# A two-layer diffusion backbone on one core: modulation column on TensorE, Fourier sums on VectorE, urgencies for the pieces of the first phase

## The chip, the cores and the metric

The program runs on one core of a Trainium2 chip. The metric is the device time of one execution in microseconds (us), and the lower the better. A "time" below is the median of the timed runs unless it is called the profiled execution's own.

## What is computed

The reference carries a latent stream `x` (512 tokens, width 1024) through two layers and a final norm; all is fp32.

```python
# each layer: modulated norm, mixer, gated residual; then the same with the MLP
h = modulate(rmsnorm(x, norm1_g[i]), sh1, sc1)     # h * (1 + scale) + shift
y = hybrid_ab_mixer(...) if even else fourier_mixer(h, fourier_w_out[j])
x = x + gt1 * y
x = x + gt2 * channel_mlp(modulate(rmsnorm(x, norm2_g[i]), sh2, sc2), w1[i], w2[i])
# channel_mlp: square(relu(h @ w1)) @ w2,  w1 1024 x 4096
# fourier_mixer: real part of fft2 over (tokens, 256 channels of a group), then a 1024 x 1024 map
# hybrid mixer: input projection -> windowed attention with 256 context keys, and a
#               bidirectional RWKV-7 scan (chunks of 64 tokens) -> output projection
return rmsnorm(x, final_g)
```

The shifts, scales and gates come from `silu(c) @ ada_w + ada_b`.

## The kernel before

The body does not issue instructions; it records them. A `Plan` object notes every operation (`record`), knows what each must wait for, and then orders all of them in `solve`: it steps through a model of the five engines and takes, on each engine, the ready operation with the largest urgency, which is the length of the longest chain of work behind it plus the record's `lead` (0 for all records in the kernel before). `issue` then writes the instructions in that order, so each engine runs its own list strictly in order. Where the plan's model sees TensorE wait, it puts in dummy matmuls, `warm<-identr` (L673), that keep TensorE busy. All instructions come from that one place, so nearly every row of the profile says L683; rows are told apart by their tiles.

Every fp32 product is made of three matmuls (`mm3`): an operand is split into a high part (ScalarE, `whi<-st`, `hhi<-ht`, `uhi<-x`) and the rest (VectorE, `wlo<-st,whi`, `hlo`, `ulo`). Weights arrive by SyncE's queue as 128 x 512 halves in the ring `st` (five buffers); `whi` and `wlo` have three buffers each.

The stages in order of time:

- First phase, 0 to about 560 us. A table of words, `PLAN`, lists its pieces: `tile` (a tile of the input projection, matmuls `ps<-hhi,whi`), `post`, `lora`, `ada` (columns of the modulation, made on VectorE), `prep`, `mats`, `nat`, `inv` (inversion of 64 x 64 blocks, with the small matmuls `Yt,ab`, `Vt,Zt`, `Xs,ab` and `ab,Xs`), the scan chain `u`, `s`, `y` (`vu,ab`, `zs,ab`, `vu,gq`, `St`), attention (`qry`, `max`, `row`, `attn`) and the output projection (`out`, `read`).
- Layer 0's MLP, 590 to 920 us. `norm_rows` sums the squares (`ps<-cst,sq`), makes the reciprocal root (VectorE `ms`, GpSimd `rs`) and spreads it over the partitions (`ps<-cst,rs`, ScalarE `rb`). Only then can `mod_split` make the modulated input: VectorE `ht<-x,AM,rb`, ScalarE `hhi`, VectorE `hlo`, for eight tiles of 128 channels.
- So that TensorE need not wait for that, the first `NG` tiles of the MLP take the unnormalised input (`uhi`, `ulo`) and are scaled by `rb` after their matmuls. The shift of the modulation then has to be added as a column, `w1` transposed times the shift: GpSimd multiplies the weight tile by the shift (`wb<-st,adv`), adds the eight parts up (`wb<-wb`), and TensorE sums over the partitions with one matmul against a column of ones (`ps<-cst,wb`); ScalarE copies the result to `wbs`.
- The Fourier layer, 920 to 1018 us. `fw_load` makes the sum `wa` (GpSimd) and the difference `wb` (VectorE) of two weight halves, `fw_split` splits both; `PF` is how many output tiles ahead they are made. For each of eight output tiles, ScalarE makes `qg` from one product, GpSimd subtracts and adds it to the residual (`xn<-xn,qg`), VectorE adds the other product (`x<-ps,adv,xn`), and ScalarE and VectorE split the result for the MLP.
- Layer 1's MLP, from 1018 us, in which `last` makes the final norm in two halves of 256 tokens: eight products `o<-y,rb` a half, of which GpSimd makes those of `PLM`.

Of the kernel before, what the change touches and what calls it, by code (L numbers as in the profile page):

```python
# [8 lines left out]
ALU = mybir.AluOpType  # L9
# [229 lines left out]
class Plan:  # L239
# [11 lines left out]
    def __init__(self, nc):  # L251
        self.nc = nc
        for e in self.ENGS:
            setattr(self, e, Queue(self, e))
        self.recs, self.pools, self.closed = [], [], []
        self.tiles, self.hist, self.preds, self.soft = {}, {}, [], []
        self.ahead, self.piece = 0, 0


    def tile_pool(self, **kw):  # L260
# [431 lines left out]
def body(tc, I, out):  # L692
# [4 lines left out]
    act, dve, pool, pe = nc.scalar, nc.vector, nc.gpsimd, nc.tensor  # L697
# [22 lines left out]
    ones1 = K("ones")  # L720
# [638 lines left out]
    y = {}  # L1359
# [399 lines left out]


    PLAN = """
    tile 0, tile 1, post 0, lora 0, tile 2, post 1, lora 1, tile 3, post 2, lora 2, tile 4, post 3, lora 3, tile 5,
    ada 2, post 4, prep 0 0, ada 4, prep 0 1, tile 6, post 5, mats 0 0, mats 0 1, nat 0 0, nat 0 1,
    inv 0, tile 7, ada 6, post 6, tile 8, ada 8, post 7, ada 10, tile 9, tile 10, ada 12, post 8, post 9, tile 11,
    ada 14, post 10, tile 12, ada 16, post 11, rope, tile 14, post 12, prep 1 0, prep 1 1,
    mats 1 0, mats 1 1, nat 1 0, nat 1 1, tile 15, post 14, inv 1, tile 16, ada 18, post 15,
    prep 2 0, prep 2 1, mats 2 0, mats 2 1, nat 2 0, tile 17, ada 20, post 16, tile 18, ada 22,
    tile 19, post 17, inv 2, post 18, ada 24, nat 2 1, tile 13, post 19, post 13, kv, u 0 0, s 0 0,
    u 0 1, s 0 1, prep 3 0, prep 3 1, u 1 0, s 1 0, mats 3 0, mats 3 1, nat 3 0,
    nat 3 1, inv 3, qry 0, max 0 0, u 1 1, max 0 1, row 0, s 1 1, prep 4 0,  # L1770
    bonus 2, prep 4 1, mats 4 0, mats 4 1, nat 4 0, nat 4 1, inv 4, ed 2 0,
    ed 2 1, u 2 0, s 2 0, y 2 0, u 2 1, s 2 1, y 2 1, prep 5 0, prep 5 1, mats 5 0, mats 5 1, nat 5 0, inv 5,
    attn 0, bonus 3, ed 3 0, ed 3 1, u 3 0, s 3 0, y 3 0, u 3 1, s 3 1, y 3 1, qry 1,
    max 1 0, max 1 1, row 1, u 4 0, s 4 0, ed 4 0, ed 4 1, y 4 0, bonus 4, u 4 1, attn 1,
    qry 3, max 3 0, ed 5 1, y 4 1, s 4 1, u 5 0, s 5 0, ed 5 0, max 3 1, row 3,
    bonus 5, y 5 0, u 5 1, y 5 1, attn 3, qry 2, max 2 0, max 2 1, row 2, attn 2, out 0,
    out 1, out 2, out 3, out 4, out 5, out 6, out 7, read 4, read 5, read 3, read 2
    """
# [55 lines left out]
    def tq(name, shape=(128, 512)):  # L1834
        return h2("E", shape=shape, name=name)


    NG = 3
    PF = 3
    AXE = 1  # L1840

    def mlp(l, xs, ai, sh, gt, nxt):

        us = US[:]
        US.clear()

        rb = norm_rows(Q, SQ, T, "rk")
        gs = []
        for f in range(NG):
            st = load(I["w1"][l, f])  # L1850
            pr = [tq("wb") for u in range(2)]
            for u in range(2):
                b = adv[:, sh + 4 * u : sh + 4 * u + 4].unsqueeze(2).to_broadcast([128, 4, 128])
                pool.tensor_tensor(pr[u].rearrange("p (k c) -> p k c", k=4), st[u].rearrange("p (k c) -> p k c", k=4), b, ALU.mult)
            w = split_w(st)
            p = pst("ch" if f < 2 else "iv")
            for k in range(8):
                mm3(p, w, k, us[k], k == 0, k == 7)
            pool.tensor_tensor(pr[0], pr[0], pr[1], ALU.add)
            for n in (256, 128):  # L1860
                pool.tensor_tensor(pr[0][:, 0:n], pr[0][:, 0:n], pr[0][:, n : 2 * n], ALU.add)
            pb = pst("rk")
            pe.matmul(pb[:, 0:1], pr[0][:, 0:128], ones1, start=True, stop=True)
            wb = Q.tile([128, 1], F32, tag="wbs", bufs=NG, name="wbs")
            act.copy(wb, pb[:, 0:1])
            gs.append((p, wb))
        hs = []
        for k in range(8):
            hi, lo = hq("hhi"), hq("hlo")
            mod_split(Q, xs[k], rb, AM[:, ai, k : k + 1], adv[:, sh + k : sh + k + 1], hi, lo, T)  # L1870
            hs.append((hi, lo))
        for half in range(2):
            zs = []
            for f in range(16):
                if l == 0:
                    ada_bg(24 + max(0, 32 * half + f - 3) * 56 // 60)
                r = tq("r")
                if half == 0 and f < NG:
                    dve.tensor_tensor(r, gs[f][0], rb, ALU.mult)
                    act.activation(r, r, AF.Relu, bias=gs[f][1])  # L1880
                else:
                    w = split_w(load(I["w1"][l, 16 * half + f]))
                    p = pst("mm")
                    for k in range(8):
                        mm3(p, w, k, hs[k], k == 0, k == 7)
                    act.activation(r, p, AF.Relu)
                s = tq("s")
                act.activation(s, r, AF.Square)
                hi, lo = zq("zhi"), zq("zlo")
                act.copy(hi, s)  # L1890
                dve.tensor_tensor(lo, s, hi, ALU.subtract)
                zs.append((hi, lo))
            nx = []
            for m in range(8):
                if l == 1 and half == 1 and m == 6:
                    ws = [wk for kh in range(2) for wk in split_w(load(I["w2"][l, half, 7, kh]), True)]
                if l == 1 and half == 1 and m == 7:
                    return last(ws, zs, xs[m], adv[:, gt + m : gt + m + 1])
                p = pst("mm")
                for kh in range(2):  # L1900
                    if l == 0:
                        ada_bg(24 + (32 * half + 13 + 2 * m + kh) * 56 // 60)
                    w = split_w(load(I["w2"][l, half, m, kh]))
                    for k in range(8):
                        mm3(p, w, k, zs[8 * kh + k], kh == 0 and k == 0, kh == 1 and k == 7)
                xn = xt("xn")
                dve.scalar_tensor_tensor(xn, p, adv[:, gt + m : gt + m + 1], xs[m], ALU.mult, ALU.add)
                nx.append(xn)
                if half == 1:
                    nxt(xn, m)  # L1910
            xs = nx
        return xs
# [33 lines left out]
    def fw_load(m):  # L1946
        st = load(I["fw"][m])
        wa, wb = h2("ed", name="wa"), h2("ed", name="wb")
        pool.tensor_tensor(wa, st[0], st[1], ALU.add)
        dve.scalar_tensor_tensor(wb, st[0], K("onez"), st[1], ALU.mult, ALU.subtract)  # L1950
        return wa, wb

# [86 lines left out]
    for m in range(8):  # L2039
        if m + PF < 8:  # L2040
            fou["w", m + PF] = fw_load(m + PF)
            fw_split(m + PF)
        w = fou["ws", m]
        pq, pp = pst("mm"), pst("mm")
        for g in range(4):
            mm3(pq[:, 0:256], w, 4 + g, U[g][1], g == 0, g == 3)
        for g in range(4):
            mm3(pp[:, 0:258], w, g, U[g][0], g == 0, False)
        ms = slice(128 * (m % 4), 128 * (m % 4) + 128)
        fxh, fxl = fx[m // 4]  # L2050
        pe.matmul(pp[:, 0:258], fxh[:, ms], uxh, start=False, stop=False)
        pe.matmul(pp[:, 0:258], fxh[:, ms], uxl, start=False, stop=False)
        pe.matmul(pp[:, 0:258], fxl[:, ms], uxh, start=False, stop=True)
        gt = adv[:, 48 + m : 49 + m]
        qg = tq("qg", (128, 256))
        act.activation(qg, pq[:, 0:256], AF.Copy, scale=gt)
        xr = x2[m]
        pool.tensor_tensor(xr[:, 1:256], xr[:, 1:256], qg[:, 1:256], ALU.subtract)
        pool.tensor_tensor(xr[:, 257:512], xr[:, 257:512], qg[:, 255:0:-1], ALU.add)
        xn = xt("x3")  # L2060
        dve.scalar_tensor_tensor(xn[:, 0:256], pp[:, 0:256], gt, xr[:, 0:256], ALU.mult, ALU.add)
        dve.scalar_tensor_tensor(xn[:, 256:512], pp[:, 256:0:-1], gt, xr[:, 256:512], ALU.mult, ALU.add)
        x3.append(xn)
        scaled(xn, 2, m)
# [45 lines left out]
                dmae[q % 2].dma_start(out[g * q : g * q + g, :, c].rearrange("m p t -> p m t"), o)  # L2110

    PARTS = ((0, 256), (256, 256))
    PLM = (0, 2, 4)
    mlp(1, x3, 2, 56, 72, pre_final)
    p2.close()
    es.close()
# [20 lines left out]
```

## Time and profile before

| | |
|---|---|
| median of 3 timed runs | 1395.5 us (1393.81 to 1397.6) |
| profiled execution's own time | 1390.24 us |
| its span | 1388.5 us |
| mean granted TensorE clock | 0.971 |
| TensorE busy (matmul) | 1319.0 us, 95% |
| VectorE busy | 837.4 us, 60% |
| ScalarE busy | 613.2 us, 44% |
| GpSimd busy | 161.6 us, 12% |

The share of TensorE counts the dummy matmuls as busy, and matmuls that run at a lower clock count longer. So its 95% does not say that 5% is all there is to gain. The stretches are read one by one.

### The profile page before, as it was taken

The numbers are of one execution on the slowest core, as the hardware profiler recorded it, in microseconds if no ns is written. First come the engines' busy times: TensorE is split into PE (matmuls) and PEld (weight loads), VectorE is DVE, ScalarE is ACT, GpSimd is POOL, SyncE is SP. The second block draws the span as 40 slices with busy tenths as digits, with TensorE's granted clock in tenths as the row PEclk, the third lists the DMA queues.
The fourth block names the chain that finished last, engine by engine and source line by source line (L and its number), as shares of the span: only waits on it lengthen the run. The fifth ranks groups of instructions, "written<-read, shape, count | busy, mean of one in ns | idle before, by whom it ended". The sixth has DMA issues, their size and how long they took to land.

```text
span 1388.5 us, 27641 instructions
## 1 busy us (share of the span) xinstructions
PE 1319.0 (95%) x10824; PEld 1084.8 (78%) x10824; DVE 837.4 (60%) x1702; ACT 613.2 (44%) x1193; POOL 161.6 (12%) x219
## 2 busy tenths in 40 slices
PE   6999997789898999999999999999999999999997
PEld 2888885577777778778887888889978888888886
DVE  2874987678676456867555565675865332333334
ACT  3674744175533334537422455334537522355332
POOL 1420101122010111040000000000550000000001
PEclk9999997789998999999999999999999999999998
DMA  9488876746636113236655556570322333233222
GB/s 364 161 239 259 284 206 182 202 113 188 170 92 166 60 50 118 69 100 220 187 182 186 178 192 189 189 232 19 102 69 89 94 99 100 91 99 98 96 88 76
DMA packets 173938, 204.69 MB, mean 147 GB/s; under 512 B 52008, under 2 KB 87912, under 8 KB 173808
## 3 DMA queue, kind: packets, MB, share of 16 engines
q1 hardware_dynamic: 171920, 200.99, 46.8%
q8 instruction: 85, 1.39, 0.4%
q10 hardware_dynamic: 1376, 1.90, 0.4%
q14 instruction: 45, 0.37, 0.1%
q0 software_dynamic: 512, 0.03, 0.0%
HBM read 177.41 MB, written 25.43 MB: 146 GB/s over the span
## 4 chain that ended last, share of the span: by engine, by line
PE 57%; DVE 1%; DMA 1%; ACT 0%; issue 0%; POOL 0%; DVEq 0%; ACTq 0%
PE ps L683 55%; PE warm L673 1%; DMA st<-adaB_in 1%; DVE wlo L683 1%; DVE ht L683 0%; DVE st L683 0%; DVE o L683 0%; POOL o L683 0%; DVE xn L683 0%; ACT hhi L683 0%; ACT whi L683 0%; DVEq L2132 0%; ACT rb L683 0%; POOL rs L683 0%; DVE adv L683 0%
## 5 line engine op out<-in xcount | busy, mean ns | idle before, releaser
L683 ACT CAST whi<-st 128x512 fp32r<-128x512 f32 x306 | 188.2, 620 | 426.1 <-PE ps L683 365.6
L683 DVE TENSOR_TENSOR wlo<-st,whi 128x512 fp32r<-128x512 f32 x306 | 213.2, 707 | 213.4 <-ACT whi L683 154.4
L683 PE MATMUL ps<-hhi,whi 128*128 128x512 f32 x600 | 232.8, 399 | 7.6 <-ACT wbs L683 3.8
L683 PE MATMUL ps<-hlo,whi 128*128 128x512 f32 x600 | 230.7, 395 | 0.0
L683 PE MATMUL ps<-hhi,wlo 128*128 128x512 f32 x600 | 230.3, 398 | 0.0
L683 PE MATMUL ps<-zhi,whi 128*128 128x512 f32 (+1 forms) x528 | 200.2, 383 | 0.0
L683 PE MATMUL ps<-zlo,whi 128*128 128x512 f32 (+1 forms) x528 | 199.7, 383 | 0.0
L683 PE MATMUL ps<-zhi,wlo 128*128 128x512 f32 (+1 forms) x528 | 196.1, 384 | 1.8 <-DVE wlo L683 1.7
L683 PEld LDWEIGHTS ps<-hhi,whi 128*128 128x128 f32 x600 | 114.1, 191 | 34.2 <-ACT whi L683 5.7
L683 PEld LDWEIGHTS ps<-hhi,wlo 128*128 128x128 f32 x600 | 114.1, 190 | 23.9 <-DVE ab L683 0.5
L683 PEld LDWEIGHTS ps<-hlo,whi 128*128 128x128 f32 x600 | 114.0, 190 | 23.1 <-issue 0.9
L683 PEld LDWEIGHTS ps<-zhi,wlo 128*128 128x128 f32 x528 | 98.9, 188 | 22.7 <-DVE wlo L683 3.4
L683 PEld LDWEIGHTS ps<-zhi,whi 128*128 128x128 f32 x528 | 98.9, 188 | 20.0 <-ACT whi L683 0.7
L683 PEld LDWEIGHTS ps<-zlo,whi 128*128 128x128 f32 x528 | 99.1, 188 | 19.3
L683 DVE CUSTOM_DVE_ANT_0 st<-st,sB,vec 128x512 f32<-128x512 f32 x56 | 42.0, 750 | 44.2 <-DMA st<-adaB_in 43.8
L683 DVE TENSOR_TENSOR zlo<-s,zhi 128x512 fp32r<-128x512 f32 x64 | 43.9, 690 | 27.2 <-ACT zhi L683 27.2
L683 POOL TENSOR_TENSOR rs<-ms,pw 128x4 f32<-128x4 f32 (+1 forms) x7 | 6.2, 885 | 406.6 <-DVE ms L683 406.6
L683 POOL TENSOR_TENSOR wa<-st 128x512 f32<-128x512 f32 x8 | 11.6, 1452 | 341.2 <-DMA st<-fw_in 320.9
L683 DVE CUSTOM_DVE_ANT_0 st<-st,sB,adv 128x512 f32<-128x512 f32 x56 | 41.9, 748 | 9.3 <-DMA st<-adaB_in 8.4
L683 PE MATMUL ps<-pr,gq 64*128 64x128 f32 (+1 forms) x384 | 35.5, 302 | 6.6 <-DVE gq L683 5.1
L683 PEld LDWEIGHTS ps<-pr,gq 64*128 64x128 f32 x384 | 32.2, 206 | 11.3 <-issue 8.0
L683 ACT ACTIVATE s<-r 128x512 f32<-128x512 f32 x64 | 40.7, 636 | 0.6
(398 smaller groups left out, 2430.6 us busy)
## 6 DMA issues: line engine op xcount, KB each, us to landing
st<-w_in SPq DMA_DIRECT2D x256, 256.0 KB, 2.8
st<-adaB_in SPq DMA_DIRECT2D x112, 256.0 KB, 3.1
ada<-adaB_in SPq DMA_DIRECT2D x48, 256.0 KB, 3.9
st<-win_in SPq DMA_DIRECT2D x40, 256.0 KB, 4.2
spl_th<-th SPq DMA_DIRECT2D x16, 384.0 KB, 4.0
pgth<-spl_th SPq DMA_DIRECT2D x24, 256.0 KB, 4.8
st<-adaA_in SPq DMA_DIRECT2D x16, 256.0 KB, 5.0
st<-adaA_in SPq DMA_DIRECT2D x8, 512.0 KB, 7.5
```

What stands on the lines that cost most here:

```text
L673: i = tc.nc.tensor.matmul(p, i, i.unsqueeze(1).to_broadcast([128, 4, 128]), start=True, stop=True)
L683: i = getattr(getattr(tc.nc, r.eng), r.op)(*[tr(a) for a in r.args], **{x: tr(a) for x, a in r.kw.items()})
```

## The change

- `NG` 3 becomes 2: two tiles of each MLP, not three, use the unnormalised input. Their column is made by TensorE alone: eight matmuls `ps<-adv,st` (weights 128 x 128 as stationary operand, one column of the shift moving) instead of GpSimd's products and sums and one matmul.
- `PF` 3 becomes 4: the Fourier weights are made one output tile further ahead.
- The sum `wa` of `fw_load` and the two updates of the residual by `qg` move from GpSimd to VectorE.
- `PLM` becomes empty: all products of the final norm are on VectorE.
- The words of `PLAN` may carry a lead in us ("post 8:25.8"), which is added to the urgency of that piece's records. Some forty words carry one, between -60.6 and 27.2. What is recorded ahead of the table has a lead of 56.7 us, what comes behind it none.

```diff
-        self.ahead, self.piece = 0, 0
+        self.ahead, self.piece = 56700, 0
...
-    prep 2 0, prep 2 1, mats 2 0, mats 2 1, nat 2 0, tile 17, ada 20, post 16, tile 18, ada 22,
+    post 15, prep 2 0, prep 2 1, mats 2 0, mats 2 1:1.0, nat 2 0, tile 17, ada 20, post 16, tile 18, ada 22, tile 19,
...
     for piece in PLAN.replace("\n", " ").split(","):
-        what, *args = piece.split()
-        tc.piece += 1
+        what, _, lead = piece.strip().partition(":")
+        what, *args = what.split()
+        tc.piece, tc.ahead = tc.piece + 1, round(1000 * float(lead or 0))
         WORK[what](*map(int, args))
...
-    NG = 3
-    PF = 3
+    NG = 2
+    PF = 4
...
         for f in range(NG):
             st = load(I["w1"][l, f])
-            pr = [tq("wb") for u in range(2)]
-            for u in range(2):
-                b = adv[:, sh + 4 * u : sh + 4 * u + 4].unsqueeze(2).to_broadcast([128, 4, 128])
-                pool.tensor_tensor(pr[u].rearrange("p (k c) -> p k c", k=4), st[u].rearrange("p (k c) -> p k c", k=4), b, ALU.mult)
             w = split_w(st)
...
-            pool.tensor_tensor(pr[0], pr[0], pr[1], ALU.add)
-            for n in (256, 128):
-                pool.tensor_tensor(pr[0][:, 0:n], pr[0][:, 0:n], pr[0][:, n : 2 * n], ALU.add)
             pb = pst("rk")
-            pe.matmul(pb[:, 0:1], pr[0][:, 0:128], ones1, start=True, stop=True)
+            for k in range(8):
+                pe.matmul(pb[:, 0:1], st[k // 4][:, 128 * (k % 4) : 128 * (k % 4) + 128], adv[:, sh + k : sh + k + 1], start=k == 0, stop=k == 7)
...
-        pool.tensor_tensor(wa, st[0], st[1], ALU.add)
+        dve.tensor_tensor(wa, st[0], st[1], ALU.add)
...
-        pool.tensor_tensor(xr[:, 1:256], xr[:, 1:256], qg[:, 1:256], ALU.subtract)
-        pool.tensor_tensor(xr[:, 257:512], xr[:, 257:512], qg[:, 255:0:-1], ALU.add)
+        dve.tensor_tensor(xr[:, 1:256], xr[:, 1:256], qg[:, 1:256], ALU.subtract)
+        dve.tensor_tensor(xr[:, 257:512], xr[:, 257:512], qg[:, 255:0:-1], ALU.add)
...
-    PLM = (0, 2, 4)
+    PLM = ()
```

What this does to the order is seen at four places. The first is VectorE at the start of layer 0's MLP, where `ms` is the mean of the squares and `ht` the first step of the modulated input. Before:

```order
L683 SCALAR_TENSOR_TENSOR ulo<-xo,AM,uhi 128x512
L683 TENSOR_SCALAR ms<-ps 128x4
L683 TENSOR_TENSOR wlo<-st,whi 128x512 x5
L683 SCALAR_TENSOR_TENSOR ht<-xo,AM,rb 128x512 x3
L683 SCALAR_TENSOR_TENSOR hlo<-ht,adv,hhi 128x512
```

And after:

```order
L683 TENSOR_SCALAR ms<-ps 128x4
L683 SCALAR_TENSOR_TENSOR ulo<-xo,AM,uhi 128x512
L683 TENSOR_TENSOR wlo<-st,whi 128x512
L683 SCALAR_TENSOR_TENSOR ht<-xo,AM,rb 128x512 x3
L683 SCALAR_TENSOR_TENSOR hlo<-ht,adv,hhi 128x512
```

Between the mean and the first `ht` stood five splits of weights; now one stands there, and one `ulo`.

The second is TensorE a little later at the same place: `uhi` and `ulo` belong to the tiles on the unnormalised input, `hhi` and `hlo` to the first tile on the modulated one. Before:

```order
L683 MATMUL ps<-uhi,wlo 128x512
L673 MATMUL warm<-identr 128x512 x12
L683 MATMUL ps<-cst,wb 128x1
L683 MATMUL ps<-hhi,whi 128x512 x2
L673 MATMUL warm<-identr 128x512 x8
L683 MATMUL ps<-hlo,whi 128x512
```

And after:

```order
L683 MATMUL ps<-ulo,whi 128x512
L683 MATMUL ps<-uhi,wlo 128x512
L683 MATMUL ps<-hhi,whi 128x512
L683 MATMUL ps<-uhi,whi 128x512
L683 MATMUL ps<-hlo,whi 128x512
L683 MATMUL ps<-ulo,whi 128x512
L683 MATMUL ps<-hhi,wlo 128x512
L683 MATMUL ps<-adv,st 128x1
L683 MATMUL ps<-uhi,wlo 128x512
L683 MATMUL ps<-hhi,whi 128x512
```

The matmuls on the modulated input now stand between the last ones on the unnormalised input and the new column matmuls; the dummies are gone here. At the start of layer 1's MLP it is the same picture. Ahead of the rows shown, 16 matmuls on `uhi` and `ulo` and 8 of the column stand between the last `ps<-cst,rs` and the first `ps<-hhi,whi`.

The third is VectorE in the Fourier layer, at the first output tiles (`xn<-xn,qg` is the update of the residual). Before:

```order
L683 TENSOR_TENSOR uxl<-ps,uxh 4x258
L683 TENSOR_TENSOR fxl<-fst,fxh 4x512
L683 SCALAR_TENSOR_TENSOR wb<-st,cst 128x512
L683 TENSOR_TENSOR fxl<-fst,fxh 4x512
L683 TENSOR_TENSOR fwlo<-wa,fwhi 128x512
L683 SCALAR_TENSOR_TENSOR x_11566<-ps,adv,xn 128x256
```

And after:

```order
L683 TENSOR_TENSOR uxl<-ps,uxh 4x258
L683 TENSOR_TENSOR xn<-xn,qg 128x255 x2
L683 TENSOR_TENSOR fxl<-fst,fxh 4x512
L683 TENSOR_TENSOR wa<-st 128x512
L683 TENSOR_TENSOR fxl<-fst,fxh 4x512
L683 TENSOR_TENSOR xn<-xn,qg 128x255 x2
L683 SCALAR_TENSOR_TENSOR wb<-st,cst 128x512
L683 TENSOR_TENSOR fwlo<-wa,fwhi 128x512
L683 SCALAR_TENSOR_TENSOR x_11512<-ps,adv,xn 128x256
```

What GpSimd did stands in VectorE's list now. Of the dummies, 36 stood on TensorE in this layer up to its end (in groups of 7, 9, 8, 9 and 3); now 14 do (3, 10 and 1).

The fourth is TensorE in the first phase, at the end of the second inversion (`Xs,ab` and then `ab,Xs`), where the scan chain starts (`zs,ab`, `vu,gq`, `vu,ab`). Before:

```order
L683 MATMUL ps<-vu,gq 64x64 x16
L683 MATMUL ps<-vu,ab 64x64 x16
L683 MATMUL ps<-Xs,ab 32x32 x32
L683 MATMUL ps<-St_3372,pr 64x64 x16
L683 MATMUL ps<-hlo,whi 128x512
L683 MATMUL ps<-hhi,wlo 128x512
L683 MATMUL ps<-cst,vc 128x128 x2
L683 MATMUL ps<-cst,vl 128x128 x4
L683 MATMUL ps<-zs,ab 64x64 x16
L683 MATMUL ps<-ab,Xs 32x32 x32
```

And after:

```order
L683 MATMUL ps<-Xs,ab 32x32 x32
L683 MATMUL ps<-hhi,wlo 128x512
L683 MATMUL ps<-hhi,whi 128x512
L683 MATMUL ps<-hlo,whi 128x512
L683 MATMUL ps<-hhi,wlo 128x512
L683 MATMUL ps<-ab,Xs 32x32
L683 MATMUL ps<-vu,ab 64x64 x16
L683 MATMUL ps<-qz,cst 128x512
L683 MATMUL ps<-ab,Xs 32x32 x31
L683 MATMUL ps<-zs,ab 64x64 x16
```

Before, 480 of the projection's matmuls `hhi`/`hlo` with 512 columns stood ahead of the inversion's last product, which is all of them; now 459 do, so 21 are left to run behind it. The first 580 rows of TensorE's list are the same in both.

More of the change, by code (lines that the diff above doesn't have):

```diff
@@ L1761, in body @@
     PLAN = """
[L1762 to L1766, printed above, removed]
@@ L1767, in body @@
-    prep 2 0, prep 2 1, mats 2 0, mats 2 1, nat 2 0, tile 17, ada 20, post 16, tile 18, ada 22,
[L1768 to L1777, printed above, removed]
+    tile 0, tile 1:-1.6, post 0, lora 0, tile 2, post 1, lora 1, tile 3:3.8, post 2, lora 2, tile 4, post 3:-1.5,
@@ new lines, in body @@
+    lora 3, tile 5, ada 2, post 4, prep 0 0, ada 4:12.8, prep 0 1, tile 6, post 5, mats 0 0, mats 0 1, nat 0 0:-0.2,
+    nat 0 1:-11.4, inv 0, tile 7, ada 6:-1.7, post 6, tile 8, ada 8, post 7, ada 10, tile 9, tile 10, ada 12:4.0,
+    post 8:25.8, post 9, tile 11:2.0, ada 14, post 10:14.0, tile 12, ada 16, post 11:12.5, rope:4.2, tile 14,
+    post 12, prep 1 0, prep 1 1, mats 1 0, mats 1 1, nat 1 0, nat 1 1, tile 15, post 14, inv 1:8.0, tile 16, ada 18,
+    post 15, prep 2 0, prep 2 1, mats 2 0, mats 2 1:1.0, nat 2 0, tile 17, ada 20, post 16, tile 18, ada 22, tile 19,
@@ new lines, in body @@
+    post 17, inv 2, post 18, ada 24, nat 2 1, tile 13, post 19, post 13, kv:1.9, u 0 0, s 0 0, u 0 1, s 0 1,
+    prep 3 0, prep 3 1, u 1 0, s 1 0, mats 3 0, mats 3 1, nat 3 0, nat 3 1, inv 3, qry 0, max 0 0, u 1 1, max 0 1,
+    row 0, s 1 1, prep 4 0, bonus 2, prep 4 1, mats 4 0:-29.1, mats 4 1, nat 4 0, nat 4 1, inv 4, ed 2 0:-60.6,
+    ed 2 1:-32.9, u 2 0, s 2 0:1.9, y 2 0, u 2 1, s 2 1, y 2 1, prep 5 0, prep 5 1:-4.5, mats 5 0, mats 5 1:1.5,
+    nat 5 0, inv 5, attn 0, bonus 3, ed 3 0:-32.9, ed 3 1:-32.9, u 3 0, s 3 0, y 3 0, u 3 1, s 3 1, y 3 1, qry 1,
@@ L1778, in body @@
+    max 1 0:1.2, max 1 1, row 1, u 4 0, s 4 0, ed 4 0:-32.9, ed 4 1:-32.9, y 4 0, bonus 4:-1.8, u 4 1, attn 1,
+    qry 3:-8.8, max 3 0, ed 5 1:-32.9, y 4 1, s 4 1, u 5 0, s 5 0:15.3, ed 5 0:-32.9, max 3 1, row 3:15.2, bonus 5,
+    y 5 0:27.2, u 5 1, y 5 1:-4.7, attn 3, qry 2, max 2 0, max 2 1, row 2, attn 2, out 0, out 1:9.5, out 2:-4.9,
+    out 3, out 4, out 5, out 6:5.3, out 7, read 4, read 5, read 3, read 2
     """
     for piece in PLAN.replace("\n", " ").split(","):
-        what, *args = piece.split()
```

## The prediction

> **What bounds the kernel now.** I read the page first, then its slices, then the busy time stretch by stretch, then single stretches in order of time.
>
> ```profile
> span 1388.5 us, 27641 instructions
> PE 1319.0 (95%) x10824; PEld 1084.8 (78%) x10824; DVE 837.4 (60%) x1702; ACT 613.2 (44%) x1193; POOL 161.6 (12%) x219
> PEclk9999997789998999999999999999999999999998
> PE ps L683 55%; PE warm L673 1%; DMA st<-adaB_in 1%; DVE wlo L683 1%; DVE ht L683 0%; DVE st L683 0%; DVE o L683 0%; POOL o L683 0%; DVE xn L683 0%; ACT hhi L683 0%; ACT whi L683 0%; DVEq L2132 0%; ACT rb L683 0%; POOL rs L683 0%; DVE adv L683 0%
> ```
>
> TensorE (PE) bounds: it is busy for 95%, and the chain that ended last is nearly all its matmuls, as far back as the view follows it. So whatever leaves other engines idle is free, and a change gains only what TensorE waits, fills with dummies, or runs at a low granted clock. The clock row shows where it is low: slices 7 to 9, some 210 to 310 us, and again 14. The next rows are the busy time in five stretches (length, matmul, weight load, VectorE, ScalarE, GpSimd, granted clock, DMA), and then the dummies alone in three of them.
>
> ```profile
> 210.00:310.00 100.00, 77.44 (x1609) 63.32 (x1609) 74.49 (x175) 45.44 (x97) 19.54 (x32) 0.77 0.61 170
> 310.00:480.00 170.00, 153.93 (x3165) 125.91 (x3164) 123.11 (x328) 70.30 (x156) 21.15 (x48) 0.93 0.49 139
> 590.00:613.00 23.00, 21.93 (x103) 17.86 (x102) 12.92 (x15) 5.76 (x11) 17.17 (x16) 1.00 0.33 104
> 967.00:1018.00 51.00, 51.00 (x355) 46.30 (x354) 43.14 (x66) 28.15 (x64) 24.30 (x22) 1.00 0.23 73
> 1018.00:1042.00 24.00, 21.30 (x105) 17.55 (x106) 15.01 (x18) 5.86 (x11) 17.15 (x16) 1.00 0.30 99
> ```
>
> ```profile
> 590.00:613.00 23.00, 6.92 (x26) 4.87 (x26) 1.00 0.33 104
> 967.00:1018.00 51.00, 9.26 (x36) 6.68 (x36) 1.00 0.23 73
> 1018.00:1042.00 24.00, 5.31 (x19) 3.56 (x19) 1.00 0.30 99
> ```
>
> The last three stretches look full in the first table and are not: 81 of the 136 dummies stand there. They are the starts of both MLPs and the Fourier layer, which the named edits touch. In the first two the idle share is 22.6 and 16.1 us, and the low clock takes 0.23 of 77.4 and 0.07 of 153.9 us, 17.8 and 10.8 us: 67 us in all. Only the order of the pieces touches those.
>
> **Starts of the MLPs.** Layer 0's, in order of time (start, length, what, and the wait before it in brackets):
>
> ```profile
> 596.16 0.59 ACT L683 COPY rb<-ps 128x512 f32<-128x512 f32 x1 [3.21 <-PE ps L683]
> 600.11 1.31 PE L673 MATMUL warm<-identr 128*128 128x512 f32 x5
> 601.26 0.39 PE L683 MATMUL ps<-uhi,whi 128*128 128x512 f32 x1
> 603.48 5.27 POOL L683 TENSOR_TENSOR wb<-wb 128x128 f32<-128x128 f32 x6
> 604.62 1.80 DVE L683 TENSOR_TENSOR wlo<-st,whi 128x512 fp32r<-128x512 f32 x1 [2.01 <-ACT whi L683]
> 606.35 2.94 DVE L683 SCALAR_TENSOR_TENSOR ht<-xo,AM,rb 128x512 f32<-128x512 f32 x3
> 608.11 0.73 PE L683 MATMUL ps<-hhi,whi 128*128 128x512 f32 x2 [1.07 <-ACT wbs L683]
> 1026.68 0.59 ACT L683 COPY rb<-ps 128x512 f32<-128x512 f32 x1 [6.92 <-PE ps L683]
> 1034.04 3.75 DVE L683 SCALAR_TENSOR_TENSOR ht<-x,AM,rb 128x512 f32<-128x512 f32 x3
> 1036.59 0.73 PE L683 MATMUL ps<-hhi,whi 128*128 128x512 f32 x2 [2.70 <-ACT wbs L683]
> ```
>
> Five dummies take the 1.15 us from 600.11 to 601.26: 0.23 us each. So layer 0's start loses 26 x 0.23 + 1.07 = 7.05 us and layer 1's 19 x 0.23 + 2.70 = 7.07 us. The cause is in the rows: `rb` is ready at 596.75, the first `ht` starts at 606.35, because VectorE's list has the splits of the third tile's weights ahead of it, and these wait for buffers that TensorE frees late, and run beside GpSimd's `wb`. Undisturbed a split takes 0.69 us (row further down), here 1.80.
>
> After the change one `wlo` stands ahead of `ht`. From `rb` to the first `hhi` it needs one `wlo`, one `ht` and one `hhi` (0.69 + 0.75 + 0.72, from rows here and below) and their hand-overs, some 2.5 us; the list has 16 matmuls at 0.23 and 8 columns there, 3.7 us and more. I take both waits as gone, **-14.1 us**, and put **+2.0** against it, one wait of the size of the smaller one seen (1.07) at each start, because each step of the eight costs VectorE two operations (1.4 us) and the third tile has `wlo` of its own to wait for. Between 0 and all 14.1 of it may stay.
>
> The columns cost TensorE time. The nearest rows are matmuls of the same form, a 128 x 128 fp32 stationary operand and one moving column, each shown as two passes:
>
> ```profile
> 1017.82 0.95 PE L683 MATMUL ps<-cst,sq 128*128 128x1 f32 x8
> 1018.63 0.48 PE L683 MATMUL ps<-ulo,whi 128*128 128x512 f32 x1
> ```
>
> Eight passes take 0.81 us, so one such matmul 0.20. There are 8 x 2 a layer instead of 3: 26 more in all, **+5.3 us**. If they fell into waits they would cost 0; if each cost as much as a big one (0.23), 6.0. Since I take the waits as gone, they count in full. That GpSimd loses its 17 us at each start gains nothing by itself, since nobody but `wbs` waited for it. One tile fewer on the unnormalised input moves 24 matmuls a layer from `uhi` to `hhi`: the same number at the same price. The copy `wbs` now waits for the eighth column, and on ScalarE the fourth `hhi` is queued behind the first `wbs`; in the list the columns stand early enough for that.
>
> **Fourier layer.** The groups of VectorE and GpSimd there (shape, count, busy us, mean ns, idle before), and two undisturbed ones of VectorE for comparison:
>
> ```profile
> L683 DVE SCALAR_TENSOR_TENSOR wb<-st,cst 128x512 f32<-128x512 f32 x6 | 8.0, 1341 | 0.2
> L683 DVE SCALAR_TENSOR_TENSOR ulo<-x,AM,uhi 128x512 fp32r<-128x512 f32 x8 | 7.6, 954 | 1.9 <-ACT uhi L683 1.9
> L683 DVE TENSOR_TENSOR fwlo<-wa,fwhi 128x512 fp32r<-128x512 f32 x8 | 6.4, 802 | 1.0 <-ACT fwhi L683 1.0
> L683 DVE TENSOR_TENSOR u<-ps,u 128x256 fp32r<-128x256 f32 x4 | 1.6, 406 | 0.0
> L683 DVE SCALAR_TENSOR_TENSOR ulo<-xn,AM,uhi 128x512 fp32r<-128x512 f32 x2 | 1.5, 751 | 1.3 <-ACT uhi L683 1.3
> L683 DVE TENSOR_TENSOR wlo<-st,whi 128x512 fp32r<-128x512 f32 x89 | 60.4, 690 | 109.0 <-ACT whi L683 78.7 <-PE ps L683 30.2
> L683 POOL TENSOR_TENSOR xn<-xn,qg 128x255 f32<-128x255 f32 x16 | 15.5, 989 | 12.9 <-ACT qg L683 12.9
> L683 POOL TENSOR_TENSOR wa<-st 128x512 f32<-128x512 f32 x6 | 9.0, 1506 | 23.9 <-DVE fwlo L683 16.8 <-DMA st<-fw_in 3.6 <-DVE fxl L683 3.5
> ```
>
> Beside GpSimd, VectorE's operations on two tiles in SBUF run long: 6 x (1.34 - 0.75) + 8 x (0.95 - 0.75) + 8 x (0.80 - 0.69) = 6.0 us, and smaller groups about 1 more. That falls away. Added are 6 x 0.69 for `wa` and 16 x 0.41 for the residual (`u`, the nearest of this size): 10.6 us. VectorE's 43.1 of 51 us become 46.7. TensorE's real work there is 51 - 36 x 0.23 = 42.7. So the list saves 22 dummies (36 less 14), 5.1 us, but VectorE has 46.7 us to do and waits at the end for the last products, as it does now. I take half, **-2.5 us**. At best it is -5.1. At worst the 12.9 us that GpSimd waited for `qg` become waits of VectorE's list, with the splits `fwlo` and the sums `x` queued behind them: +8. `PF` 4 makes one pair of weights earlier from the same `st` buffers; its loads run while SyncE has little to bring (DMA 0.23 busy), so it is nothing by itself.
>
> **The end.**
>
> ```profile
> 1376.17 2.29 DVE L683 TENSOR_TENSOR o<-y,rb 128x256 f32<-128x256 f32 x3
> 1377.80 0.42 ACT L683 ACTIVATE sq<-xn 128x256 f32<-128x256 f32 x1 [2.40 <-DVE o L683]
> 1381.81 3.01 DVE L683 TENSOR_TENSOR o<-y,rb 128x256 f32<-128x256 f32 x4 [2.52 <-ACT rb L683]
> 1384.75 0.47 DVE L683 SCALAR_TENSOR_TENSOR o<-xn,vec,rb 128x256 f32<-128x256 f32 x1
> ```
>
> Four products take 3.01 us beside GpSimd's three. Seven alone, at 0.41 for one of this size less the 0.08 by which neighbours overlap, are 2.4: **-0.5 us** at the end. In the first half the square `sq` stands on ScalarE behind an output transfer that waits for the first four products; `xn` and four products on VectorE end about where GpSimd's did, so it is nothing there (0.5 either way).
>
> **The order of the first phase.** It is the term I can price least. Between 210 and 310 us the chain of inversions and scan steps waits for VectorE and for hand-overs:
>
> ```profile
> 220.00:230.00 10.00, 8.48 (x91) 6.75 (x90) 5.65 (x18) 6.04 (x16) 0.00 (x0) 0.67 0.43 145
> 230.00:240.00 10.00, 5.86 (x84) 5.31 (x84) 9.84 (x25) 3.73 (x9) 0.00 (x0) 0.67 0.53 161
> 234.14 2.64 PE L683 MATMUL ps<-pr,gq 64*128 64x128 f32 x16 [4.88 <-DVE gq L683]
> ```
>
> The work is the same and no operation is cheaper; the new order pulls the end of the second inversion ahead of 21 projection matmuls, which then fill TensorE while the next step of the chain is under way: 21 x 0.23 = **-4.8 us**. Bounds: a third of the 67 us, -20, and +10, two more waits such as the one of 4.88. I take the small one since the first 200 us keep their order and the later inversions change places but little.
>
> **Sum.** -14.1 + 2.0 + 5.3 - 2.5 - 0.5 - 4.8 = -14.6 us on the profiled execution's own 1390.24 us (its span and 1.7 around it), 1375.6. The median of the runs is 5.3 above that execution, so 1380.9: **1381 us**.
>
> **Rivals.**
> *The order gives much more.* For it: 67 us are there, and VectorE, with 74.5 of 100 us, is not full. Against it: the same chain with the same latencies. At -20 instead of -4.8: 1366 us.
>
> *The waits at the MLP starts stay in another form.* `st` has five buffers. Now four of them stay taken until TensorE has done the columns from them, so the third tile's loads come later:
>
> ```profile
> st<-w_in SPq DMA_DIRECT2D x256, 256.0 KB, 2.8
> ```
>
> A late half costs 2.8 for the landing, and 0.6 and 0.7 for `whi` and `wlo`, 4.1 us; with the eight steps behind it 5 to 6 a start. Against it: some 45 rows of TensorE's list, about 9 us, lie between the fourth column and the matmuls that need this half. If it happens at both starts: 1381 + 11 = 1392 us, and the change is a wash.
>
> *Slower: the first phase falls into the low clock more often.* In the row of 220 to 230 us, 8.48 us of matmuls at 0.67 lose 2.8 and the idle rest 1.5: 4.3 us in ten. Without the gain of the order the sum is 1386; it passes 1400 from the fourth more such stretch on, and four give 1403. For it: the new list has 21 dummies in one place in the middle of the phase, so a wait of about 5 us is expected even there. Against it: the kernel before has 20 in the same part. [...]
>
> **How the numbers follow.** The forecast has 0.52, the better order 0.20, the late loads 0.16, the low clock 0.09; 0.03 is for what I have not seen. A difference under 0.3%, 4.2 us, is about what a measurement cannot tell from none, so faster means below 1391.3 and slower above 1399.7. Forecast and better order lie below, and so does a quarter of the third case: 0.77. Same takes the rest of it: 0.13; slower the low clock and one half of the unseen: 0.10. The range reaches from the better order, 1364, to the far side of the late loads, 1396; the forecast's own bounds lie in it (-5.1 and +8 for Fourier, all 14.1 of the starts not at once).
>
> **What would show it.** Right: dummies at both MLP starts near none, `ht` within 3 us of `rb`, a split at 0.7 us there, `ps<-adv,st` at 0.2 us each; VectorE at 45 us or more of the Fourier stretch and that stretch 2 to 3 us shorter; the end of the first phase (the first `ulo`) about 5 us earlier. Wrong: a wait of TensorE on `whi` or `wlo` of the third tile, a stretch as long as before with VectorE waiting for `qg`, or a first phase that ends more than 8 us away from where it should.

## The result, and the profile after

The changed kernel takes 1378.4 us (median of 4, 1375.5 to 1386.5) against 1395.1 us, a ratio of 0.9897 (95% interval 0.9867 to 0.9927). The forecast was 1381. The profiled execution's own time is 1379.87 us, 10.4 below that of before. A second set of runs of the same kernel, made with the last experiments, gave 1377.6 us and 0.9870 (0.9840 to 0.9901).

The page of the changed kernel, the rows that stand for those shown of before:

```profile
span 1378.1 us, 27531 instructions
PE 1323.2 (96%) x10811; PEld 1080.5 (78%) x10811; DVE 829.3 (60%) x1730; ACT 616.1 (45%) x1191; POOL 96.9 (7%) x159
PEclk9999998889998999999999999999999999999999
PE ps L683 44%; DMA st<-w_in 1%; DMA st<-adaB_in 1%; DVE wlo L683 0%; DMA st<-fw_in 0%; PE warm L673 0%; DVE o L683 0%; DVE st L683 0%; ACT whi L683 0%; DVE xn L683 0%; POOLq L2128 0%; POOL rs L683 0%; DVE wa L683 0%; DVE wb L683 0%; DVEq L2128 0%
```

TensorE is busy 4 us *longer* than before, although some 65 dummies are gone from it and the program is shorter. That does not fit a change that only takes waits away, and it is the first thing to explain.

Busy time by stretch, with the columns as before (length, matmul, weight load, VectorE, ScalarE, GpSimd, clock, DMA), and then the dummies alone in the last three:

```profile
210.00:310.00 100.00, 86.08 (x1891) 71.22 (x1891) 81.29 (x198) 48.60 (x106) 20.33 (x34) 0.81 0.60 165
310.00:480.00 170.00, 156.08 (x3188) 125.16 (x3188) 116.51 (x309) 67.61 (x145) 21.19 (x48) 0.91 0.50 138
576.00:599.00 23.00, 23.00 (x131) 19.85 (x130) 20.14 (x32) 13.76 (x25) 1.46 (x1) 1.00 0.26 77
959.00:1001.00 42.00, 42.00 (x320) 39.24 (x318) 39.39 (x82) 24.90 (x62) 0.00 (x0) 1.00 0.26 83
1001.00:1025.00 24.00, 24.00 (x134) 20.72 (x133) 21.04 (x34) 12.86 (x23) 1.32 (x1) 1.00 0.29 87
```

```profile
576.00:599.00 23.00, 0.00 (x0) 1.00 0.26 77
959.00:1001.00 42.00, 3.66 (x14) 1.00 0.26 83
1001.00:1025.00 24.00, 0.13 (x1) 1.00 0.29 87
```

Both MLP starts are full of real work, at a granted clock of 1.00 (the one dummy of the last row ends the Fourier layer). The start of layer 0 in order of time:

```profile
583.63 0.59 ACT L683 COPY rb<-ps 128x512 f32<-128x512 f32 x1 [2.29 <-PE ps L683]
583.66 0.28 PE L683 MATMUL ps<-adv,st 128*128 128x1 f32 x2
584.25 2.08 DVE L683 SCALAR_TENSOR_TENSOR ht<-xo,AM,rb 128x512 f32<-128x512 f32 x3 [2.18 <-ACT rb L683]
585.03 1.39 ACT L683 ACTIVATE hhi<-ht,adv 128x512 fp32r<-128x512 f32 x2 [0.82 <-DVE ht L683]
588.26 0.69 DVE L683 TENSOR_TENSOR wlo<-st,whi 128x512 fp32r<-128x512 f32 x1
588.92 0.40 PE L683 MATMUL ps<-hhi,whi 128*128 128x512 f32 x1
```

`ht` follows `rb` at once (583.63 + 0.59, then 584.25); before it came 9.6 us later.

Where the 10.4 us came from, by the start times of the same matmuls in the two traces:

| stretch | before | after | difference |
|---|---|---|---|
| start to the first `rwhi` (output projection) | 561.7 | 552.4 | -9.4 |
| to layer 0's first `zhi` | 115.9 | 113.5 | -2.5 |
| to layer 0's last `zhi` | 268.3 | 273.3 | **+5.0** |
| to layer 1's first `zhi` (Fourier layer, second start) | 160.4 | 150.6 | -9.9 |
| to the last norm's first sum | 264.8 | 272.2 | **+7.4** |
| to the end | 17.2 | 16.2 | -1.1 |

Nine matmuls of the output projection (`mhi`, `mlo`; 2.1 us) have moved from the first row into the second. The two bold rows are the bodies of the MLPs, in which the change edits nothing: there 12.4 of some 23 us gained are lost again. 1.7 us of that are one wait, in layer 1, for a weight half that lands late (ScalarE's split of it, `whi`, had stood 5.34 us for the transfer `st<-w_in`); a wait of 1.5 us at this place is in the second profile of the same kernel too.

```profile
1342.66 0.50 PE L683 MATMUL ps<-zhi,whi 128*128 128x512 f32 x1 [1.67 <-ACT whi L683]
```

Nearly all the rest is a longer step, that is, a longer distance from the start of one matmul to the start of the next. Here are 80 us in which TensorE does nothing but layer 1's second product (`zhi`, `zlo` moving, `whi` and `wlo` stationary), and 60 us of its first product (`hhi`, `hlo`): length, TensorE's busy time and number of matmuls, clock, DMA. Before:

```profile
1118.00:1198.00 80.00, 80.00 (x354) 1.00 0.30 98
1205.00:1265.00 60.00, 60.00 (x266) 1.00 0.33 101
```

After:

```profile
1101.00:1181.00 80.00, 80.00 (x345) 1.00 0.29 96
1192.00:1252.00 60.00, 60.00 (x267) 1.00 0.31 97
```

Nine matmuls fewer in the same 80 us, with TensorE never idle and the clock at 1.00; none fewer in the other product. As the mean distance of neighbouring starts in the four stretches of `z` matmuls it is 0.2268 us before and 0.2333 after; for `h` it is 0.2268 or 0.2269 in both. Of the 1584 `z` matmuls 1488 have 512 columns; at 6.5 ns more they make 9.7 us. The other 96, in layer 1's last halves, have 256 columns and show no difference: 0.1245 us before, 0.1244 after. (The 0.2245 and 0.2167 us for layer 1 in the next text are means that take these 96 in.)

### The profile page after: what moved, and what is told of

Its sections match the earlier page's. It is cut to its first block, busy times and chain, and to the rows that moved or that the text cites. A ratio compares the mean times of both kernels' runs of the same rounds, so it can differ in the third digit from the quotient of the medians.

```text
span 1378.1 us, 27531 instructions
## 1 busy us (share of the span) xinstructions
PE 1323.2 (96%) x10811; PEld 1080.5 (78%) x10811; DVE 829.3 (60%) x1730; ACT 616.1 (45%) x1191; POOL 96.9 (7%) x159
## 5 line engine op out<-in xcount | busy, mean ns | idle before, releaser
L683 DVE TENSOR_TENSOR wlo<-st,whi 128x512 fp32r<-128x512 f32 x306 | 207.8, 689 | 228.7 <-ACT whi L683 168.8
L683 PE MATMUL ps<-hhi,whi 128*128 128x512 f32 x616 | 237.7, 396 | 1.6 <-ACT whi L683 1.0
L683 PE MATMUL ps<-hlo,whi 128*128 128x512 f32 x616 | 235.3, 393 | 0.0
L683 PE MATMUL ps<-hhi,wlo 128*128 128x512 f32 x616 | 233.5, 395 | 0.1
L683 PE MATMUL ps<-zhi,whi 128*128 128x512 f32 (+1 forms) x528 | 204.0, 390 | 2.0 <-ACT whi L683 2.0
L683 PE MATMUL ps<-zlo,whi 128*128 128x512 f32 (+1 forms) x528 | 203.3, 390 | 0.0
L683 PE MATMUL ps<-zhi,wlo 128*128 128x512 f32 (+1 forms) x528 | 200.0, 391 | 1.8 <-DVE wlo L683 1.7
L683 PEld LDWEIGHTS ps<-hhi,whi 128*128 128x128 f32 x616 | 116.0, 189 | 27.2 <-ACT whi L683 2.2
L683 DVE TENSOR_TENSOR zlo<-s,zhi 128x512 fp32r<-128x512 f32 x64 | 44.2, 692 | 28.5 <-ACT zhi L683 28.4
L683 PE MATMUL ps<-pr,gq 64*128 64x128 f32 (+1 forms) x384 | 38.7, 323 | 2.2 <-issue 2.2
L683 ACT CAST zhi<-s 128x512 fp32r<-128x512 f32 x64 | 39.6, 621 | 1.4
L683 PEld LDWEIGHTS ps<-pr,gq 64*128 64x128 f32 x384 | 35.0, 225 | 6.6 <-issue 5.5
```

The source lines that it names most:

```text
L683: i = getattr(getattr(tc.nc, r.eng), r.op)(*[tr(a) for a in r.args], **{x: tr(a) for x, a in r.kw.items()})
```

## Experiments

What differs for these matmuls in the program is where the tiles lie. The pool that holds `zhi` and `zlo` begins with a pad, some small tiles, and the `NG` tiles `wbs`, and each of these takes 32 bytes of a partition. With two `wbs` instead of three, all `z` tiles lie 32 bytes lower. In the two built programs the lowest is at byte 149632, a multiple of 64, where it was at 149664. The weights `whi` stay at 40864, 42912 and 44960, and `hhi` too is at 32 past a multiple of 64.

**The pad, both ways.** The edit, in the changed kernel and in the kernel before:

```diff
-                    pools[name].tile([128, 8], F32, name="zpad")
+                    pools[name].tile([128, 16], F32, name="zpad")
```

> The changed kernel with 32 bytes more of padding ahead of the second half's tiles in SBUF; every engine's list is the same. In the trace of the changed kernel the matmul steps on zhi and zlo take 0.2338 and 0.2245 us in the two MLP layers, against 0.2273 and 0.2167 before, 4.8 + 6.4 us in all, while the steps on hhi and hlo keep theirs. Theory A (place): two wbs tiles instead of three put all z tiles 32 bytes lower, and that makes the step longer; with the padding the z steps are back at 0.226 and the time falls by some 11 us, to about 1367. Theory B (company): the z steps are slower because of something else that runs or is granted there; the padding changes nothing, 1378.

> The kernel before with the same 32 bytes of padding; every engine's list is the same. Theory A (place): the z tiles now lie where the changed kernel has them, the z steps go from 0.226 to 0.233 us, 1584 of them, and the time rises by 10 to 11 us, to about 1406. Theory B (company): no change, 1395.

The changed kernel with the pad takes 1370.1 us, ratio to before 0.9836 (0.9805 to 0.9867); the kernel before with the pad 1402.4 us, 1.0051 (1.0031 to 1.0072). The 80 us of `z` matmuls again, the changed kernel with the pad:

```profile
1099.00:1179.00 80.00, 80.00 (x355) 1.00 0.30 99
```

and the kernel before with the pad:

```profile
1131.00:1211.00 80.00, 80.00 (x344) 1.00 0.29 96
```

The step follows the pad in both directions, so theory A holds: place, not company. In time it is 7 to 8 us by the medians either way, a little less than the 9.7 of the steps; that still lies within the interval of the kernel before with the pad, 4.3 to 10.0 us. The padded kernel beats both kernels.

**Which place?** The first run keeps the pad and moves everything from the weight pool on by another 32 bytes, so that the `z` tiles are again where the weights are modulo 64; the second has no pad ahead of `z` alone and moves only the pool of `hhi`, `uhi` and `rwhi` and what lies behind it, and leaves the weights.

```diff
+            if p.name == "wp":                              # second run: "H"
+                pools["wp"].tile([128, 8], F32, name="hpad")   # second run: pools["H"]
```

> The changed kernel with its z tiles as with the padding, and 32 bytes of padding ahead of all weights, hhi, uhi and rwhi tiles too, so that everything lies 32 bytes higher and the z tiles, the weights and the other operands all stand at multiples of 64 bytes. Theory A1 (relative place): a step is slow where the moving tile and the weights differ by 32 bytes within 64; here none does, all steps are at 0.226, time about 1367. Theory A2 (absolute place): a step is slow where the moving tile stands at a multiple of 64; here all do, so the z steps stay at 0.233 and the h, u and r steps, some 1640 of the second phase alone, go from 0.227 to 0.233 too, time about 1390. Theory B (company): 1378.

> The changed kernel with 32 bytes of padding ahead of the pool that holds hhi, hlo, uhi, ulo, rwhi, rwlo and the modulated tiles, and no other: these go to multiples of 64 bytes, the z tiles behind them to 32 past one, the weights whi and wlo stay at 32 past one. Theory W (the partner is the weights that TensorE reads): z steps 0.2268, h and r steps 0.2333, since these now differ from the weights. Theory H (the partner is the tiles that VectorE and ScalarE write in that pool): z steps stay at 0.2333, h and r steps at 0.2268. The time says little: under W 1640 steps lose 10.7 us and 1584 gain 10.3, about 1378 in both.

Everything shifted: 1371.0 us, 0.9835 (0.9808 to 0.9863), as fast as with the pad alone, though the moving tiles and weights of the MLPs now all start at multiples of 64:

```profile
1098.00:1178.00 80.00, 80.00 (x355) 1.00 0.30 99
1187.00:1247.00 60.00, 60.00 (x266) 1.00 0.30 97
```

Weights apart: 1375.5 us, 0.9867 (0.9822 to 0.9912), with the parts exchanged. `z` is fast (354) and `h` slow (259 in 60 us, where all others have 266 or 267); their steps are 0.2269 and 0.2333:

```profile
1101.00:1181.00 80.00, 80.00 (x354) 1.00 0.31 99
1190.00:1250.00 60.00, 60.00 (x259) 1.00 0.30 93
```

So A1 and W: what counts is how the moving tile lies to the stationary weights, not where either lies, and not what VectorE and ScalarE write. In the fast cases the two starts are a multiple of 256 bytes apart, in the slow ones 32 bytes more or less than that. That the same place within 64 bytes is enough is not shown.

**The order alone.** The kernel before with the urgencies only, and the padded kernel without them:

```diff
-        self.ahead, self.piece = 0, 0
+        self.ahead, self.piece = 56700, 0
...
-    tile 0, tile 1, post 0, lora 0, tile 2, post 1, lora 1, tile 3, post 2, lora 2, tile 4, post 3, lora 3, tile 5,
+    tile 0, tile 1:-1.6, post 0, lora 0, tile 2, post 1, lora 1, tile 3:3.8, post 2, lora 2, tile 4, post 3:-1.5,
```

> The kernel before with the urgencies of the first phase's pieces alone. By the forecast's term -4.8 us, by the accounts of the two traces (start of the output projection 9.4 us earlier, of which 2.1 are projection matmuls put off) -7.3 us: about 1388. Rival: the gain in the first phase is no property of the order but of the run, or hangs on the later edits; then 1393 to 1397.

> The changed kernel with the 32 bytes of padding, but the first phase without its urgencies, as before. The order alone gave 9.7 us on the kernel before. If the terms add up: 1370 + 9.7, about 1380. By the forecast's term (4.8): 1375. Rival: with the column and the Fourier layer changed the order is worth nothing more, 1370 to 1372.

Alone: 1385.4 us, 0.9932 (0.9906 to 0.9958), so 5.9 to 13.1 us gained. Taken away: 1379.4 us, 0.9878 (0.9850 to 0.9906), 9.3 above the padded kernel's median, which is of another set (5.9 by the two ratios). The gain is in the first phase, where the forecast put it. The stretch of 210 to 310 us of the kernel before with the order:

```profile
210.00:310.00 100.00, 87.60 (x1959) 72.13 (x1959) 81.33 (x204) 48.38 (x107) 20.32 (x34) 0.83 0.61 170
```

and of the padded kernel without it:

```profile
210.00:310.00 100.00, 80.18 (x1620) 65.79 (x1620) 74.38 (x177) 45.86 (x99) 19.72 (x32) 0.76 0.62 170
```

Idle time 12.4 against 19.8 us (22.6 in the kernel before), and the clock 0.83 against 0.76. Some 350 matmuls more than in the kernel before are done in the same 100 us, and all but two of them have fewer than 512 columns: those of 512 are 96 in the kernel before and 98 with the order. So it is the chain that moves forward, and not the projection that fills its waits. The last product of the second inversion, in the kernel before and then with the order alone:

```profile
289.31 1.10 PE L683 MATMUL ps<-ab,Xs 32*32 32x32 f32 x58
```

```profile
264.19 1.19 PE L683 MATMUL ps<-ab,Xs 32*32 32x32 f32 x62
```

One trace of the first phase says little about its length, but all fourteen traces agree. The first `rwhi` starts between 561.7 and 572.3 us in the seven with the old order and between 547.6 and 555.1 in the seven with the new one, and TensorE is idle ahead of it for 51.1 to 56.5 us against 42.6 to 46.6.

**The column and the tiles.** The change does two things at the MLP starts, two tiles instead of three and the column by TensorE; three runs part them, all on the kernel before (where it has two tiles, with the pad).

```diff
-    NG = 3                          # two tiles only; both
+    NG = 2
...
-            pb = pst("rk")          # column only; both
-            pe.matmul(pb[:, 0:1], pr[0][:, 0:128], ones1, start=True, stop=True)
+            pb = pst("rk")
+            for k in range(8):
+                pe.matmul(pb[:, 0:1], st[k // 4][:, 128 * (k % 4) : 128 * (k % 4) + 128], adv[:, sh + k : sh + k + 1], start=k == 0, stop=k == 7)
```

> The kernel before with the column by TensorE and two tiles instead of three, and padding so that the z tiles keep their place. Forecast's terms: -14.1 + 2.0 + 5.3 = -6.8, about 1388. Accounts of the two traces: 47 dummies and 3.8 us of idle time at the starts go (14.6), 32 columns come for 6 (5 to 7 with the slower neighbours): -9, about 1386. Rival: the columns take as much as the waits give, 1393 to 1397.

> The kernel before with the column by TensorE, but still three tiles. Theory L (VectorE's list: the splits of the third tile stand ahead of ht): the third tile is still there, so waits or dummies of some 5 us stay at each start, and 42 more columns at 0.20 cost 8.4: 1395 to 1400. Theory G (GpSimd: its 17 us of products make wbs late and stretch VectorE's operations): both starts are free of dummies, -14.6 + 8.4 = -6: about 1389; rb to the first hhi under 6 us.

> The kernel before with two tiles instead of three, the columns still on GpSimd, and the padding. Theory L (VectorE's list: the third tile's splits): with that tile gone the waits go, -14: about 1381. Theory G (GpSimd): its work shrinks by a third, the waits stay at some 20 dummies a start and the cover is a tile shorter: 1393 to 1400.

| | us | ratio | interval |
|---|---|---|---|
| both | 1383.1 | 0.9918 | 0.9895 to 0.9941 |
| column by TensorE, three tiles | 1387.6 | 0.9944 | 0.9925 to 0.9963 |
| two tiles, column by GpSimd | 1389.8 | 0.9969 | 0.9946 to 0.9992 |

The dummies at the two starts, column by TensorE and three tiles:

```profile
587.00:610.00 23.00, 0.00 (x0) 1.00 0.26 80
1013.00:1037.00 24.00, 0.00 (x0) 1.00 0.27 83
```

Two tiles and GpSimd, and then layer 0's `rb`, two splits and `ht` of this run:

```profile
584.00:607.00 23.00, 5.88 (x20) 1.00 0.22 69
1016.00:1040.00 24.00, 4.46 (x17) 1.00 0.32 99
```

```profile
591.04 0.59 ACT L683 COPY rb<-ps 128x512 f32<-128x512 f32 x1 [2.27 <-PE ps L683]
594.08 2.33 DVE L683 TENSOR_TENSOR wlo<-st,whi 128x512 fp32r<-128x512 f32 x2 [4.58 <-PE ps L683]
596.33 3.78 DVE L683 SCALAR_TENSOR_TENSOR ht<-xo,AM,rb 128x512 f32<-128x512 f32 x3
```

Theory G: it is GpSimd. With the third tile still there and GpSimd free, all dummies go; with the third tile gone and GpSimd kept, 37 stand in these two stretches (45 before). Taking the third tile away alone still gains 1.1 to 7.5 us, so it is not without effect; in that run GpSimd makes one column in three less, too. There too VectorE has splits ahead of `ht` that wait for TensorE, and runs long (1.17 and 1.26 us each instead of 0.69 and 0.75). That GpSimd's columns bring the waits about is shown. By which way they do it (late columns, VectorE slowed beside GpSimd, or the solved order that puts the splits first) was not tried by itself.

**The Fourier layer alone.**

```diff
-        pool.tensor_tensor(wa, st[0], st[1], ALU.add)
+        dve.tensor_tensor(wa, st[0], st[1], ALU.add)
...
-        pool.tensor_tensor(xr[:, 1:256], xr[:, 1:256], qg[:, 1:256], ALU.subtract)
+        dve.tensor_tensor(xr[:, 1:256], xr[:, 1:256], qg[:, 1:256], ALU.subtract)
...
-    PF = 3
+    PF = 4
```

> The kernel before with the Fourier sums (wa, xr) on VectorE and PF 4. Forecast -2.5 (bounds -5.1 and +8): 1392.5. By the accounts of the two traces the layer's dummies fall from 38 to 15, -5.3: about 1390. Rival: part of that came from the free GpSimd at the start of the second MLP, then -2 to 0. VectorE's operations there at 0.75, 0.75 and 0.69 us instead of 1.34, 0.95 and 0.80.

1390.1 us, 0.9965 (0.9943 to 0.9988). From the first sum of squares behind layer 0 to the spreading of the next norm it takes 73.7 us instead of 77.9, -4.2; 13 dummies stand in the layer's last 47 us, where 36 stood in 51:

```profile
971.00:1018.00 47.00, 3.66 (x13) 1.00 0.24 74
```

VectorE's groups there:

```profile
L683 DVE TENSOR_TENSOR xn<-xn,qg 128x255 f32<-128x255 f32 x16 | 6.2, 418 | 1.8 <-ACT qg L683 1.6
L683 DVE TENSOR_TENSOR fwlo<-wa,fwhi 128x512 fp32r<-128x512 f32 x8 | 5.4, 681 | 0.0
L683 DVE SCALAR_TENSOR_TENSOR ulo<-x,AM,uhi 128x512 fp32r<-128x512 f32 x7 | 5.2, 744 | 0.0
L683 DVE SCALAR_TENSOR_TENSOR wb<-st,cst 128x512 f32<-128x512 f32 x6 | 4.5, 743 | 0.0
```

With GpSimd's sums gone from this layer `wb`, `ulo` and `fwlo` take 743, 744 and 681 ns; they took 1341, 954 and 802.

**The last products.** The padded kernel with three of the seven products of each last half on GpSimd again:

```diff
-    PLM = ()
+    PLM = (0, 2, 4)
```

> The changed kernel with the padding, three of the seven products of each last half back on GpSimd. Forecast's term for moving them to VectorE: -0.5, so 1370.5; bounds 0 and -1.1 (by the two traces the stretch behind the last zlo is 12.5 us instead of 13.1). Rival: VectorE is the longer of the two at the end, 1369.

1368.2 us, 0.9799 (0.9772 to 0.9826). That overlaps the interval of the padded kernel with all products on VectorE (0.9805 to 0.9867), so no difference is shown; if there is one, it is against the edit. In the traces the end, from the start of the last `zhi` matmul on, takes 12.8 us split and 12.6 on VectorE.

**The changed kernel again**, for the comparison with the runs of the last set:

> The changed kernel once more, unaltered, beside the next ones on the same chip: 1378 (1375 to 1382). Against it the padded kernel's 1370 is read.

1377.6 us, as quoted above; its `z` steps are 0.2333 us again.

## Why the forecast was right, and where it was not

The total was right, 1378 for 1381, and the gains listed for the MLP starts, the Fourier layer and the first phase all came. That the number came so close is luck. Two errors cancelled in it: the terms that were listed gave more than was put down, and a loss of 7 to 10 us was not listed at all. The forecast also took the median to lie 5.3 us above the profiled execution, as in the kernel before; for the changed kernel it lies 1.5 below (1378.4 and 1379.9, where 1375.6 was worked out).

- **Waits at the MLP starts, -14.1, less 2.0.** No dummy and no wait is left there, so the 14.1 came in full, and the 2.0 kept back for late splits did not. The reason given was wrong. The forecast said that VectorE's list had the splits of the third tile's weights ahead of `ht`, and that GpSimd's lost 17 us gain nothing by themselves. The runs with one half of the edit each show that it is GpSimd's column work: with it gone and three tiles no dummy is left, with it kept and two tiles 37 of 45 are. With 6.2 for the columns (next item) the starts should give 7.9 us; the run with both halves gives 12.1 (8.2 to 14.6). Part of the rest is in the Fourier layer, where 29 dummies stand in that run, 7 fewer than the 36 of the kernel before (1.6 us); what the others are is open.

```profile
996.00:1016.00 20.00, 7.97 (x29) 1.00 0.25 79
```

- **Columns, +5.3 at 0.20 each.** Between big matmuls they cost more: from 583.35 to 595.36 us TensorE did 36 matmuls of 512 columns and 16 column matmuls, so (12.01 - 36 x 0.2268) / 16 = 0.24 us. 26 x 0.24 = 6.2. The third tile with its 16 columns costs 4.4 us of median (1387.6 against 1383.1).
- **Fourier layer, -2.5.** Measured alone -4.2 in its stretch, -1.7 to -8.0 in time. VectorE's durations came out as worked out (0.743, 0.744, 0.68 and 0.418 for 0.75, 0.75, 0.69 and 0.41). The step that failed is the halving: VectorE waits only 1.6 us for `qg`, where GpSimd had waited 12.9, and has other work in its list between two updates. So nearly the whole of the best case (-5.1) came.
- **The end, -0.5.** Not resolved; -0.2 in the traces of the padded kernel. Seven products on VectorE take 2.4 us as forecast:

```profile
1366.23 2.43 DVE L683 TENSOR_TENSOR o<-y,rb 128x256 f32<-128x256 f32 x7
1371.69 2.44 DVE L683 TENSOR_TENSOR o<-y,rb 128x256 f32<-128x256 f32 x7 [1.98 <-ACT rb L683]
```

- **Order, -4.8.** Measured -9.5 (-5.9 to -13.1). The second inversion does end ahead of 21 projection matmuls, as forecast, and some 25 us earlier. The step that failed is the price, 21 x 0.23: the stretch from 210 to 310 us has 98 matmuls of 512 columns where it had 96, so these do not fill it. Its idle time falls by 10 us (22.6 to 12.4) as the later steps of the chain come into it, twice what was put down.
- **What was not there.** Every matmul of the body was taken at its old price, since the edit does not touch it. `NG` also sets the number of buffers `wbs`, that moves the `z` tiles by 32 bytes, and 1488 matmuls get 6.5 ns dearer, 9.7 us.

The experiments on the kernel before add up, by medians, to -9.7 (order) - 12.1 (two tiles and column) - 5.1 (Fourier) + 7.3 (place) = -19.6 us, in which the 7 dummies of the Fourier layer that either edit removes (1.6 us) are counted twice; the change measured -16.7 in one set and -19.5 in the other. Of the rivals, the better order (-20) did not come in full; the late loads at the starts did not come at all, no wait on `whi` or `wlo` stands there; and the low clock cost about what it had: 0.19 of 86.1 and 0.09 of 156.1 us between 210 and 480 us, 30.4 us in all, against 28.6 before (busy time by the share that the granted clock lacks, an estimate in both). So the slower case did not come, and the first phase gains by less idle time (27.8 us in these stretches, 38.7 before), not by the clock. One reading of the prediction is off without effect: the second low place in its clock row is the thirteenth slice, not the fourteenth.

Of the signs named, `ht` follows `rb` in 0.03 us, a split takes 0.69 us, and the first `ulo` comes 5.7 us earlier. The columns are dearer than the 0.2 us named (0.24). VectorE in the Fourier layer, in the run with that edit alone, is busy for 44.2 of 47 us, a little under the 45 named.

## What to carry to other kernels

When TensorE's busy time rises although work was taken out, count the matmuls in equal stretches of an untouched stage: here a step longer by 3% (0.2333 us for 0.2268) showed as 345 matmuls for 354 in 80 us, in which TensorE had no idle time that a view of waits could show. Whoever changes the number or size of small buffers should compare how far the big moving operands lie from their weights before and after, and pad where that has changed; here 32 bytes are worth about half of what the whole change gave (7 to 8 us beside 16.7). And an engine that feeds one small result into a chain may hold up more than its own link: here taking GpSimd's columns away cleared both MLP starts (no dummy where 45 stood, with the third tile still there), though only `wbs` waited for their result.

## What the hardware showed that was not expected

In these runs a 128 x 512 matmul on fp32r tiles in the MLPs has a step of 0.2268 us where the moving tile and the weights start a multiple of 256 bytes apart, and 0.2333 us where the distance is 32 bytes more or less. Told by offsets within 64 bytes, the short step was measured with both at 32 (kernel before) and with both at 0 (all shifted), the long one with the moving tile at 0 and the weights at 32 (changed kernel, and kernel before with the pad: `z`; weights apart: `h`), the long one too in both MLP products; moving tiles at 32 with weights at 0 were not run in such a stream, and nor were other offsets than 0 and 32. Whether the same offset within 64 bytes is enough is open: the 72 matmuls of `hhi` and `hlo` with the weights `gh` and `gl`, from 38 to 65 us, have both tiles at 32, but an odd multiple of 128 bytes apart, and their mean step is 0.2325 us in the kernel before (47 steps between neighbours, without two of 0.32 us), at a clock of 1.00. That stretch is also busier on the other engines (VectorE 21.0 of the 24 us from 38 to 62), so the distance is not shown to be the cause. The matmuls of 256 columns show no such loss: the 96 of `z` have a step of 0.1245 us in the kernel before and 0.1244 in the changed kernel, and `ps<-d2hi,abhi` (256 and 258 columns) in the Fourier layer has 0.120 and 0.119, though of its two tiles `abhi` alone has moved. So in the MLPs the 32 bytes cost 6.5 ns for each matmul of 512 columns. What makes it so stays open.
